# Making the weight sum S4 by an accumulating transfer instead of a VectorE addition, in four pairs of a feed-forward

## The chip, the cores and the metric

The kernel runs on one core of one Trainium2 chip. The metric is the device time of one execution in microseconds (us). Shorter is better. The kernel before has a median of 1458.25 us over 3 runs (1457.26 to 1460.52).

## The reference, cut to what matters

The kernel computes a two-layer encoder trunk on 512 tokens of width 1024 in float32. Each layer is a mixer, a cross-attention to a memory of 256 tokens, and a gated feed-forward with a short causal convolution; the change touches the feed-forward alone:

```python
def conv_ffn(xn, w_up, conv_w, conv_b, w_down):
    h = causal_depthwise_conv(xn @ w_up, conv_w) + conv_b
    g, u = jnp.split(h, 2, axis=-1)
    return (jax.nn.gelu(g) * u) @ w_down
```

w_up is 1024 x 5632 (D_FF is 2816), so g and u have 22 blocks of 128 columns each. There is one such feed-forward in each of the two layers.

## The kernel before, in words

**Pairs.** The feed-forward works on 22 pairs. Pair p is block p of g with block p of u: two weight blocks, A1 and A2, of 128 x 1024 elements, each stored as two halves of 512 columns (A11 and A12, A21 and A22). Pair 0 is computed plainly (`plain`, line 1703). Pairs 1 to 21 are computed by `seven` (line 1723), a scheme with seven half-size products instead of eight, which needs sums of the weight halves: S1 = A21 + A22, S2 = A11 + S1, S4 = S2 + A12, and the sum of A11 and A21.

**Sums and splits.** The tile `sa` is loaded with A11 and A21 by SyncE's queue (line 1736), and GpSimd's queue then adds A2 onto it by an accumulating transfer (`onto`, line 1732; used at line 1737). A1 is loaded into `raw` (line 1738), A22 into `ra` (line 1739). VectorE makes S2 in a tile `sb` (line 1753) and later S4 in place, in the same tile (line 1759). Each weight that a product uses is first split into two float32r parts: ScalarE casts it (the high part, line 1747) and VectorE subtracts (the low part, line 282). S4 may be made only when both parts of S2 have been made, since it overwrites S2. Five such splits belong to a pair: w3 (A1 whole), w2 (S2), w1 (`sa` whole), w22 (A22), w4 (S4); w3 and w1 serve two products each.

**Products.** Lines 1795 to 1810 give the products P1, P5, P6, P2, P7, P3, P4. Each is 12 matmuls of 256 columns (four blocks, three matmuls each, lines 291 to 293). P3 reads S4's parts, P6 reads S2's. Between them ScalarE and VectorE pass results on: ScalarE writes P6's bank with minus P1 before P6 may start (the seed, line 1786), keeps a copy of P6 (u2, line 1790) before P7 may overwrite it, and a copy of P5 (u5); VectorE subtracts these (line 1793), P4 waiting for the subtraction after P7. A tail then scales, convolves and gates the pair: ScalarE starts the convolution (line 1669), VectorE adds two taps to each half (line 1676), ScalarE does the gelu (line 1684), VectorE the product with u (line 1686), and the result is split again (lines 1690 and 282). From pair 5 on, products of the down projection of earlier pairs are put between (`fill`).

**Buffers.** There are three `raw` and three `sa` tiles, two `sb` and two `ra` tiles, and one pair of part tiles each for S2, S4 and A22.

**What sets the order.** A planner (`Sched`, line 150) is given every step with an engine, an estimated duration, its dependencies, a due time and the buffers that it takes, and writes the steps of each engine in the order in which they come up in its plan; the framework then lays the instructions out on each engine. A transfer of `onto` counts in the plan 0.0029 us per column on GpSimd, and its data 6.0 us after that. The load of the first table of the gelu on ScalarE is no step of the plan. On the chip every engine executes its own instructions strictly in this order; an instruction whose input is missing holds up all behind it on its engine.

Of the kernel before, what the change touches and what calls it, by code (L numbers as in the profile page):

```python
# [14 lines left out]
ALU = mybir.AluOpType  # L15
# [50 lines left out]
class Plan:  # L66
# [11 lines left out]
    def add(self, fn, dur=0.0, deps=(), prio=None, take=(), free=(), chain=(), pre=(), after=0.0, order=(), load=(), st=None):  # L78
        it = Item(fn, dur, [d for d in deps if d is not None], len(self.items) if prio is None else prio, take, free, chain, pre, after, order, load, st)
        it.n = len(self.items)  # L80
        self.items.append(it)
        return it
# [154 lines left out]
class Builder:  # L237
# [1269 lines left out]
    def ffn_steps(self, layer, mp):  # L1507
# [5 lines left out]
        add = sc.add  # L1513
        tt = lambda n: 0.055 + 1.06e-3 * n
# [22 lines left out]
        def load(st, tag, src, cols, at, dur=0.0017):  # L1537
            def fn():
                to = raw_tile(st, tag)[:, :cols]
                nc.sync.dma_start(to.rearrange("p (a b) -> p a b", a=2) if len(src.shape) == 3 else to, src)  # L1540

            return add("SP", dur * cols, fn, (), at, [(tag, st)], (), 4.0)

        def parts(st, off=0):
            st["wh"], st["wl"] = self.parts(off)
# [79 lines left out]
        def small_(tag):  # L1625
            both = self.til(self.kp, tag, (P, 1088), F32R, bufs=1)
            return both[:, OFF : OFF + 512], both[:, OFF + 512 : OFF + 1024]
# [95 lines left out]
        def seven(p, fill):  # L1723
            st, sa, sb, r2, f1, f3, s2, s4, a22 = ({} for _ in range(9))
            at = clock[0]
            A1, A2 = t["up"][layer, p], t["up"][layer, 22 + p]
            tt_ = nc.vector.tensor_tensor
# [3 lines left out]
            def onto(out, src, cols, deps, due):  # L1731
                return add("POOL", 0.0029 * cols, lambda: nc.gpsimd.dma_start(out(), src(), accum_op=ALU.add), deps, due, (), (), 6.0)  # L1732

            SB = lambda: sb["sb"][:]
            soon = 40.0 if p < 5 else 0.0
            b1 = load(sa, "sa", up2[p][:, :, :512], 1024, at - 20.0 - soon, 0.0 if soon else 0.0017)
            b1 = onto(lambda: sa["sa"][:], lambda: A2, 1024, [b1], at - 16.0 - soon)
            l2 = load(r2, "raw", A1, 1024, at - 12.0)
            l1 = load(a22, "ra", A2[:, 512:], 512, at - 6.0)

            def small(s, tag):
                s["wh"], s["wl"] = small_(tag)

            def split(s, cols, deps, due, alloc, take, raw, free=()):
                def hi():
                    alloc()
                    nc.scalar.copy(s["wh"][:, :cols], raw())  # L1747

                h = add("ACT", act(cols), hi, deps, due - 3.0, take)
                return add("DVE", tt(cols), lambda: self.sub(s["wl"][:, :cols], raw(), s["wh"][:, :cols]), [h], due - 2.0, (), free)  # L1750
# [1 line left out]
            def s2_():  # L1752
                tt_(out=raw_tile(sb, "sb")[:], in0=sa["sa"][:, 512:], in1=r2["raw"][:, :512], op=ALU.add)

            b2 = add("DVE", tt(512), s2_, [b1, l2], at - 5.0, [("sb", sb)])
            w3 = split(f3, 1024, [l2], at, lambda: parts(f3, OFF), [("h", f3)], lambda: r2["raw"][:])
            w2 = split(s2, 512, [b2], at, lambda: small(s2, "s2"), [("s2", s2)], SB)
            w1 = split(f1, 1024, [b1], at + 1.0, lambda: parts(f1, OFF), [("h", f1)], lambda: sa["sa"][:])
            b4 = add("DVE", tt(512), lambda: tt_(out=SB(), in0=SB(), in1=r2["raw"][:, 512:], op=ALU.add), [w2], at - 1.5)
            w22 = split(a22, 512, [l1], at + 4.0, lambda: small(a22, "a22"), [("a22", a22)], lambda: a22["ra"][:], [("ra", a22)])  # L1760
            w4 = split(s4, 512, [b4], at + 5.0, lambda: small(s4, "s4"), [("s4", s4)], SB, [("sb", sb)])
            joined([w1, b2], at, [("sa", sa)])
# [533 lines left out]
```

## Time and profile before

| what | value |
|---|---|
| median of 3 runs (lowest to highest) | 1458.25 us (1457.26 to 1460.52) |
| the profiled execution's own time | 1458.17 us |
| its span, first to last instruction | 1456.4 us |
| matmul engine (PE) busy | 1441.7 us (99% of the span) |
| VectorE (DVE) busy | 1225.6 us (84%) |
| ScalarE (ACT) busy | 986.1 us (68%) |
| GpSimd (POOL) busy | 73.3 us (5%) |
| TensorE clock granted | 0.999 |
| transfers' share of 16 engines: SyncE's queue, GpSimd's queue | 35.1%, 10.7% |

The profiled execution's time is its span and 1.8 us around it, and lies 0.08 us under the median. Pairs 1 to 5 of the first layer lie at about 417 to 467 us of the span, those of the second layer 703.27 us later, with the same instructions. A row of a timeline gives the start in us, the duration, the engine, the line, the operation, what it writes and reads, and in brackets the idle time before it with what ended it. Starts tell more than durations: each engine begins an instruction before the one ahead has drained, so the distance of two starts is what an instruction costs when the engine is not waiting. PE's busy share hides its halts for the same reason, since the modelled end of a matmul reaches past the start of the next.

### The profile page before, as it was taken

What the parts mean: (1) busy time and instruction counts of PE and PEld (TensorE: products, weight loads), DVE (VectorE), ACT (ScalarE), POOL (GpSimd) and SP (SyncE); (2) the same over time, 40 slices, a digit from 0 to 9 for tenths busy, and PEclk for the clock granted to TensorE, in tenths of its full rate; (3) what the DMA queues carried; (4) which work ended last, traced back from release to release, by engine and by line L of the source; (5) the groups of instructions that cost most, each with busy time, mean ns of one, the idle gap of its engine ahead of it and who ended that gap; (6) DMA issues with size and microseconds to landing.
All of it is one profiled execution on the core that took longest, in us unless ns stands there. A gap on an engine that the chain in (4) does not pass through costs nothing.

```text
span 1456.4 us, 24072 instructions
## 1 busy us (share of the span) xinstructions
PE 1441.7 (99%) x9019; PEld 1279.8 (88%) x9019; DVE 1225.6 (84%) x2223; ACT 986.1 (68%) x1776; POOL 73.3 (5%) x116
## 2 busy tenths in 40 slices
PE   9999999999999999999999999999999999999998
PEld 7888787998899999999888888889988999999987
DVE  7789987867899988889669988887779998888974
ACT  7689666655677777777547665566566777777764
POOL 0001120000000000000000100000000000000000
PEclk9999999999999999999999999999999999999999
DMA  5222336752246666562233332656414666666422
GB/s 200 87 74 73 117 119 199 171 177 88 94 128 163 183 158 161 150 163 74 84 101 109 109 110 65 204 142 189 131 48 119 160 179 172 156 160 156 105 67 79
DMA packets 70628, 190.24 MB, mean 131 GB/s; under 512 B 7520, under 2 KB 7520, under 8 KB 70512
## 3 DMA queue, kind: packets, MB, share of 16 engines
q1 hardware_dynamic: 62736, 162.17, 35.1%
q0 software_dynamic: 7200, 26.22, 10.7%
q8 instruction: 70, 1.15, 0.3%
q14 instruction: 46, 0.38, 0.1%
q10 hardware_dynamic: 576, 0.33, 0.1%
HBM read 186.56 MB, written 2.13 MB: 130 GB/s over the span
## 4 chain that ended last, share of the span: by engine, by line
PE 82%; DVE 10%; ACT 4%; issue 2%; DMA 1%; POOL 0%; DVEq 0%; SPq 0%; POOLq 0%; ACTq 0%
PE acc L291 15%; PE acc L292 15%; PE acc L293 14%; PE w L293 6%; PE w L291 6%; PE w L292 6%; PE s L293 3%; PE s L291 3%; PE s L292 3%; PE acc L352 2%; PE acc L354 2%; PE acc L353 2%; DVE wl L282 2%; DMA sa<-in_xq_dram 1%; DVE x L771 1%
## 5 line engine op out<-in xcount | busy, mean ns | idle before, releaser
L282 DVE TENSOR_TENSOR wl<-raw,wh 128x1024 fp32r<-128x1024 f32 (+3 forms) x181 | 213.9, 1182 | 41.2 <-ACT wh L285 32.3
L291 PE MATMUL acc<-xh,wh 128*128 128x256 f32 (+1 forms) x624 | 206.8, 331 | 0.1
L293 PE MATMUL acc<-xh,wl 128*128 128x256 f32 (+1 forms) x624 | 205.7, 330 | 0.1
L292 PE MATMUL acc<-xl,wh 128*128 128x256 f32 (+1 forms) x624 | 205.5, 329 | 0.0
L285 ACT CAST wh<-raw 128x1024 fp32r<-128x1024 f32 (+1 forms) x123 | 126.6, 1034 | 84.6 <-PE acc L292 43.0
L1676 DVE SCALAR_TENSOR_TENSOR c<-hs,vec,c 128x512 f32<-128x512 f32 x176 | 130.5, 749 | 15.9 <-ACT c L1669 14.0
L291 PEld LDWEIGHTS acc<-xh,wh 128*128 128x128 f32 x624 | 117.2, 188 | 12.1 <-ACT v L1917 0.6
L293 PEld LDWEIGHTS acc<-xh,wl 128*128 128x128 f32 x624 | 117.1, 188 | 12.0 <-DVE wl L282 0.5
L292 PEld LDWEIGHTS acc<-xl,wh 128*128 128x128 f32 x624 | 117.2, 188 | 11.5
L293 PE MATMUL w<-ah,wl 128*128 128x512 f32 x304 | 119.1, 392 | 0.0
L292 PE MATMUL w<-al,wh 128*128 128x512 f32 x304 | 118.6, 390 | 0.0
L291 PE MATMUL w<-ah,wh 128*128 128x512 f32 x304 | 118.5, 390 | 0.0
L282 DVE TENSOR_TENSOR wl<-sa,wh 128x1024 fp32r<-128x1024 f32 x52 | 63.6, 1222 | 17.0 <-ACT wh L1747 15.6
L1669 ACT ACTIVATE c<-hs,vec 128x512 f32<-128x512 f32 x88 | 71.2, 816 | 9.6 <-DVE hs L1816 8.2
L1747 ACT CAST wh<-sa 128x1024 fp32r<-128x1024 f32 x42 | 44.0, 1049 | 35.4 <-PE w L292 30.4
L293 PEld LDWEIGHTS w<-ah,wl 128*128 128x128 f32 x304 | 57.1, 188 | 12.0
L291 PEld LDWEIGHTS w<-ah,wh 128*128 128x128 f32 x304 | 57.1, 188 | 10.0 <-ACT w L1584 0.2
L292 PEld LDWEIGHTS w<-al,wh 128*128 128x128 f32 x304 | 57.0, 188 | 9.8
L282 DVE TENSOR_TENSOR s<-sb,s 128x512 fp32r<-128x512 f32 x92 | 63.1, 686 | 2.2 <-ACT s L285 0.3
L1554 ACT CAST wh<-dr 128x512 fp32r<-128x512 f32 x64 | 39.7, 621 | 34.1 <-PE w L292 32.2
L1732 POOL DMA_DIRECT2D sa<-in_up_dram x42 | 35.9, 855 | 515.7 <-DMA sa<-in_up_dram 173.9
L291 PE MATMUL acc<-mem,wh 128*128 128x256 f32 (+1 forms) x192 | 61.5, 320 | 0.0
(534 smaller groups left out, 4667.8 us busy)
## 6 DMA issues: line engine op xcount, KB each, us to landing
raw<-in_up_dram SPq DMA_DIRECT2D x46, 512.0 KB, 3.5
sa<-in_up_dram SPq DMA_DIRECT2D x42, 512.0 KB, 4.3
sa<-in_up_dram POOLq DMA_DIRECT2D x42, 512.0 KB, 5.7
dr<-in_down_dram SPq DMA_DIRECT2D x64, 256.0 KB, 2.7
ra<-in_up_dram SPq DMA_DIRECT2D x42, 256.0 KB, 3.0
raw<-in_xk_dram SPq DMA_DIRECT2D x16, 512.0 KB, 3.6
raw<-in_wo_dram SPq DMA_DIRECT2D x16, 512.0 KB, 3.5
raw<-in_xv_dram SPq DMA_DIRECT2D x16, 512.0 KB, 3.4
```

The source lines that it names most:

```text
L282: self.nc.vector.tensor_tensor(out=lo, in0=v, in1=hi.bitcast(F32), op=ALU.subtract)
L285: self.nc.scalar.copy(hi, v)
L291: mm(out, wh, xh, start=first, stop=False, skip_group_check=parts)
L292: mm(out, wh, xl, start=False, stop=False, skip_group_check=parts)
L293: mm(out, wl, xh, start=False, stop=last, skip_group_check=parts)
L352: mm(ps, xh[k][:, ts], wh[:, ws], start=(k == 0), stop=False)
L353: mm(ps, xh[k][:, ts], wl[:, ws], start=False, stop=False)
L1554: nc.scalar.copy(st["wh"][:, :cols], st[tag][:, :cols])
L1669: nc.scalar.activation(st["c_"][:, j, :], hs()[:, j, 2:514], AF.Identity, scale=self.col("cw", (layer * 3 + 2) * 44 + blk), bias=self.col( ...
L1676: nc.vector.scalar_tensor_tensor(out=c, in0=hs()[:, j, n : n + 512], scalar=w, in1=c, op0=ALU.mult, op1=ALU.add)
L1732: return add("POOL", 0.0029 * cols, lambda: nc.gpsimd.dma_start(out(), src(), accum_op=ALU.add), deps, due, (), (), 6.0)
L1747: nc.scalar.copy(s["wh"][:, :cols], raw())
```

## The change

For pairs 2 to 5 of both layers S4 is no longer made by VectorE from `raw`; GpSimd issues an accumulating transfer that adds A12 from HBM (128 x 512 elements, 256 KB) onto S2's tile once both parts of S2 are made. In the same pairs S2, its split and S4 are due 2.0 us earlier in the plan.

```diff
+            ahead = 2.0 if p in (2, 3, 4, 5) else 0.0
-            b2 = add("DVE", tt(512), s2_, [b1, l2], at - 5.0, [("sb", sb)])
+            b2 = add("DVE", tt(512), s2_, [b1, l2], at - 5.0 - ahead, [("sb", sb)])
...
-            w2 = split(s2, 512, [b2], at, lambda: small(s2, "s2"), [("s2", s2)], SB)
+            w2 = split(s2, 512, [b2], at - ahead, lambda: small(s2, "s2"), [("s2", s2)], SB)
...
-            b4 = add("DVE", tt(512), lambda: tt_(out=SB(), in0=SB(), in1=r2["raw"][:, 512:], op=ALU.add), [w2], at - 1.5)
+            if p in (2, 3, 4, 5):
+                b4 = onto(SB, lambda: A1[:, 512:], 512, [w2], at - 1.5 - ahead)
+            else:
+                b4 = add("DVE", tt(512), lambda: tt_(out=SB(), in0=SB(), in1=r2["raw"][:, 512:], op=ALU.add), [w2], at - 1.5)
```

Behind the change line numbers from 1755 on are larger by 1 to 4 (the seed is 1790, u2 and u5 are 1794). The planner also reorders the steps around. Three places, all in the first layer; the second has the same rows.

ScalarE at pair 2, before: the cast of S4 (`s4`) stands ahead of the first pair's convolution and of pair 2's seed (`acc2`); the table load and the gelu of pair 0 (`c`) come behind the seed.

```order
L1803 COPY hs00_4587<-acc1_954_4722 128x256
L1747 CAST s4_967_4828<-sb_959_4756 128x512
L1669 ACTIVATE c_968_4832<-hs01_4588,vec_103 128x512
L1747 CAST wh_970_4849<-raw_940_4660 128x1024
L1786 ACTIVATE acc2_972_4865<-acc1_969_4834 128x256
L1684 ACT_TABLE_LOAD
L1684 ACTIVATE c_968_4832<-c_968_4832 128x512
L1810 COPY hs00_4587<-acc3_958_4754 128x256
```

ScalarE at the same place after the change, with pair 2's u5 and the cast of pair 3's S2 (`s2`) behind.

```order
L1807 COPY hs00_4587<-acc1_955_4723 128x256
L1669 ACTIVATE c_966_4828<-hs01_4588,vec_103 128x512
L1747 CAST wh_968_4845<-raw_940_4660 128x1024
L1747 CAST s4_975_4901<-sb_953_4719 128x512
L1684 ACT_TABLE_LOAD
L1684 ACTIVATE c_966_4828<-c_966_4828 128x512
L1790 ACTIVATE acc2_971_4862<-acc1_967_4831 128x256
L1794 COPY u5_973_4884<-s_970_4849 128x256
L1747 CAST s2_974_4898<-sb_961_4775 128x512
```

The cast of S4 went behind two longer steps, and the table load, the gelu and pair 2's seed now stand behind that cast. On PE, P6 of pair 2 stands after P1 and P5 of pair 2 and 8 of the 12 matmuls of P4 of pair 1.

ScalarE at pair 5 before, where `s4_1028` is S4 of pair 5, `acc3_1027` its bank of P6 (seed, then u2) and `c_1020` the tail of pair 3.

```order
L1684 ACTIVATE c_1020_5217<-c_1020_5217 128x512
L1747 CAST a22_1026_5271<-ra_999_5075 128x512
L1810 COPY hs01_4588<-acc2_1008_5139 128x256
L1786 ACTIVATE acc3_1027_5277<-acc0_1025_5258 128x256
L1747 CAST s4_1028_5292<-sb_1021_5219 128x512
L1790 COPY u2_1030_5310<-acc3_1027_5277 128x256
```

ScalarE at pair 5 after the change (`s4_1041` is S4, `acc3_1026` the bank of P6, `c_1023` the tail of pair 3).

```order
L1790 ACTIVATE acc3_1026_5256<-acc0_1022_5222 128x256
L1747 CAST s4_1041_5372<-sb_1016_5208 128x512
L1684 ACTIVATE c_1023_5235<-c_1023_5235 128x512
L1747 CAST a22_1029_5292<-ra_1004_5100 128x512
L1814 COPY hs01_4588<-acc2_1007_5120 128x256
L1794 COPY u5_1030_5309<-s_1028_5279 128x256
L1690 CAST ah_1031_5312<-c_1023_5235 128x512
L1794 COPY u2_1033_5328<-acc3_1026_5256 128x256
```

The cast of S4 moved ahead of the gelu of pair 3 and of the cast of its product, and u2 of pair 5 now stands behind all of them.

GpSimd's queue after the change; before it held the transfers onto `sa` alone, in the same order.

```order
L1732 DMA sa_949_4693<-in_up_dram 128x1024
L1732 DMA sb_953_4719<-in_up_dram 128x512
L1732 DMA sa_972_4864<-in_up_dram 128x1024
L1732 DMA sb_961_4775<-in_up_dram 128x512
L1732 DMA sa_988_4984<-in_up_dram 128x1024
L1732 DMA sb_990_5003<-in_up_dram 128x512
L1732 DMA sa_1009_5153<-in_up_dram 128x1024
L1732 DMA sb_1016_5208<-in_up_dram 128x512
```

The four new transfers (onto `sb`, pairs 2 to 5) stand between those onto `sa` of pairs 4 to 7, each of which is issued three pairs ahead.

## The prediction

> **What bounds the kernel now.** I read the page first: the engines' busy time, then the chain of work that ended last.
>
> ```profile
> PE 1441.7 (99%) x9019; PEld 1279.8 (88%) x9019; DVE 1225.6 (84%) x2223; ACT 986.1 (68%) x1776; POOL 73.3 (5%) x116
> ...
> PE 82%; DVE 10%; ACT 4%; issue 2%; DMA 1%; POOL 0%; DVEq 0%; SPq 0%; POOLq 0%; ACTq 0%
> ```
>
> The matrix engine sets the time nearly everywhere. An edit on VectorE is worth only what it takes from PE's halts, and costs only the new halts that it makes. So I cut the stretch of pairs 1 to 5 of the first layer into windows (start and end, then busy us and instructions of PE, weight loads, DVE, ACT, POOL, then the granted clock, the transfers' share and GB/s).
>
> ```profile
> 417.00:427.00 10.00, 9.80 (x86) 9.55 (x84) 8.29 (x13) 7.90 (x14) 0.88 (x1) 1.00 0.42 86
> 427.00:437.00 10.00, 9.86 (x86) 9.86 (x87) 10.00 (x15) 8.71 (x16) 0.85 (x1) 1.00 0.65 174
> 437.00:447.00 10.00, 9.59 (x84) 9.39 (x83) 10.00 (x17) 7.49 (x14) 0.86 (x1) 1.00 0.58 156
> 447.00:457.00 10.00, 9.70 (x84) 9.39 (x83) 10.00 (x15) 7.15 (x14) 0.85 (x1) 1.00 0.61 154
> 457.00:467.00 10.00, 9.89 (x77) 9.18 (x77) 10.00 (x17) 7.17 (x13) 0.86 (x1) 1.00 0.67 178
> ```
>
> From 427 on VectorE is busy without a gap while PE has lost little: here alone VectorE is as full as PE, and the halts are in PE's timeline.
>
> ```profile
> 425.27 0.28 PE L291 MATMUL acc<-xh,wh 128*128 128x256 f32 x1
> ...
> 426.52 0.28 PE L293 MATMUL acc<-xh,wl 128*128 128x256 f32 x1
> 427.14 0.39 PE L291 MATMUL acc<-kv,a 128*128 128x256 f32 x1 [0.34 <-DVE hs L1793]
> ...
> 443.47 0.28 PE L293 MATMUL acc<-kv,wl 128*128 128x256 f32 x1
> 444.15 0.38 PE L291 MATMUL s<-xh,s 128*128 128x256 f32 x1 [0.41 <-ACT u L1790]
> ...
> 448.70 0.28 PE L292 MATMUL acc<-xl,wh 128*128 128x256 f32 x1
> 449.28 0.38 PE L291 MATMUL acc<-kv,s 128*128 128x256 f32 x1 [0.30 <-ACT acc L1786]
> ...
> 459.12 0.40 PE L292 MATMUL w<-al,wh 128*128 128x512 f32 x1
> 459.63 0.39 PE L291 MATMUL acc<-kv,s 128*128 128x256 f32 x1
> ```
>
> The first two rows are the first and last matmul of one product, 11 steps: 1.25 / 11 = 0.113 us each, a product of 12 takes 1.36, and a 512-column matmul costs two steps, 0.227. Beyond that pitch the halts are 0.62 - 0.11 = 0.51, 0.68 - 0.11 = 0.57, 0.58 - 0.11 = 0.47 and 0.51 - 0.23 = 0.28. The first matmul behind a halt is also longer by 0.11 (0.39 against 0.28). Layer 0: 1.83 + 4 x 0.11 = 2.27 us. The second layer has the same places 703.27 us later; the row that differs most is the third.
>
> ```profile
> 1152.56 0.38 PE L291 MATMUL acc<-kv,s 128*128 128x256 f32 x1 [0.15 <-ACT acc L1786]
> ```
>
> It waited 0.15 less than in layer 0, so I take 2.12 for this layer: 4.39 us in both layers is what the change can win here.
>
> **What the change removes.** Four VectorE additions per layer. VectorE's rows around the first give the prices as distances of starts.
>
> ```profile
> 422.74 0.68 DVE L282 TENSOR_TENSOR s<-sb,s 128x512 fp32r<-128x512 f32 x1
> 423.34 0.68 DVE L1713 TENSOR_TENSOR hs<-acc,rb 128x512 f32<-128x512 f32 x1
> 423.94 0.68 DVE L1759 TENSOR_TENSOR sb<-sb,raw 128x512 f32<-128x512 f32 x1
> 424.54 0.42 DVE L1793 TENSOR_TENSOR hs<-s,u 128x256 f32<-128x256 f32 x1
> 424.87 0.74 DVE L1676 SCALAR_TENSOR_TENSOR c<-hs,vec,c 128x512 f32<-128x512 f32 x1
> 425.53 1.22 DVE L282 TENSOR_TENSOR wl<-sa,wh 128x1024 fp32r<-128x1024 f32 x1
> 426.67 0.42 DVE L1793 TENSOR_TENSOR hs<-acc,u 128x256 f32<-128x256 f32 x1
> ```
>
> 512 columns cost 0.60, 256 columns 0.33, a tap 0.66, a 1024-wide subtraction 1.14. A layer loses 4 x 0.60 = 2.40 us of a VectorE that is full there. That is more than each halt alone (at most 0.57), so I credit all four as gone: minus 4.39. What is late next, where they go, is the new waits.
>
> **What it adds: the transfer's landing.** No row shows a 256 KB accumulating transfer. The near ones are GpSimd's 512 KB ones (issue instruction; landing, last figure, in two windows), the queue's packets, and SyncE's plain loads.
>
> ```profile
> 418.76 0.88 POOL L1732 DMA_DIRECT2D sa<-in_up_dram  x1 [13.52 <-DMA sa<-in_up_dram]
> 431.21 0.85 POOL L1732 DMA_DIRECT2D sa<-in_up_dram  x1 [11.57 <-DVE c L1676]
> ...
> sa<-in_up_dram POOLq DMA_DIRECT2D x1, 512.0 KB, 5.4
> sa<-in_up_dram POOLq DMA_DIRECT2D x42, 512.0 KB, 5.7
> q0 software_dynamic: 7200, 26.22, 10.7%
> raw<-in_up_dram SPq DMA_DIRECT2D x46, 512.0 KB, 3.5
> ra<-in_up_dram SPq DMA_DIRECT2D x42, 256.0 KB, 3.0
> ```
>
> The first two answer to the issue at 418.76 and to all 42. Below, it cannot be less than half of 5.4, 2.7 us; above, a transfer twice as large takes 5.7. Between: q0's packets took 0.107 x 16 x 1456.4 / 7200 = 0.35 us; one transfer is 128 of them (26.22 MB / 7200 is 3.6 KB, and 512 KB are 128 rows of 4 KB), 8 per engine, 2.8 us. Half the bytes save half of that, 1.4, so 5.4 - 1.4 = **4.0 us**; I take it, and call it d. SyncE's rows, where half the size saves only 0.5, say 4.9. GpSimd itself waited 13.5 and 11.6 us ahead of the transfers shown and these are issued three pairs ahead, so the four new issues of some 0.9 us delay nothing.
>
> [...]
>
> **First new wait: P6 of pair 2.** ScalarE before, at that place:
>
> ```profile
> 424.78 0.62 ACT L1747 CAST s<-sb 128x512 fp32r<-128x512 f32 x1
> 425.31 0.82 ACT L1669 ACTIVATE c<-hs,vec 128x512 f32<-128x512 f32 x1
> 426.02 1.04 ACT L1747 CAST wh<-raw 128x1024 fp32r<-128x1024 f32 x1
> 426.96 0.37 ACT L1786 ACTIVATE acc<-acc 128x256 f32<-128x256 f32 x1
> 427.35 1.28 ACT L1684 ACT_TABLE_LOAD   x1
> 428.64 0.64 ACT L1684 ACTIVATE c<-c 128x512 f32<-128x512 f32 x1
> 429.18 0.35 ACT L1810 COPY hs<-acc 128x256 f32<-128x256 f32 x1
> 429.43 0.62 ACT L1747 CAST a<-ra 128x512 fp32r<-128x512 f32 x1
> ```
>
> Starts give: cast 0.53, convolution 0.71, wide cast 0.94, seed 0.39, table load 1.29, gelu 0.54, copy 0.25. After the change the S4 cast comes third, so ScalarE reaches it at 424.78 + 0.71 + 0.94 = 426.4. Its input: S2's low part ends at 422.74 + 0.68 = 423.42; I put 0.3 from there to the issue (an estimate: GpSimd is idle, and one semaphore lies between), and d: 427.72. Behind the cast are queued the table load, the gelu and then the seed that P6 needs: 0.53 + 1.29 + 0.54 + 0.39 = 2.75, and 0.2 for two semaphores (an estimate, between nothing and the 0.3 above): P6 could start at 430.65. PE gets there at 426.52 + 0.11 + 1.36 (P5 of pair 2) + 8 x 0.113 (of P4 of pair 1) = 428.9. PE waits 1.75 + 0.11 = **1.86 us**.
>
> **Second: P7 of pair 5.** It needs u2, which stands behind the S4 cast of pair 5. There is one buffer for S2's parts, so the S2 cast of pair 3 waits for the end of P6 of pair 2, 430.65 + 1.36 = 432.0, and its subtraction starts at 432.7. From there to the end of S2's subtraction of pair 5 stand 33 VectorE rows that I take as back to back (busy 10.00 of 10.00 above): 14 x 0.60 + 7 x 1.14 + 8 x 0.66 + 4 x 0.33 = 23.0: 455.8. Issue and landing: 460.1. Then ScalarE's row of cast 0.53, gelu 0.54, cast of A22 0.53, copy 0.25, u5 0.25, cast of the product 0.53, u2 0.25 and again 0.2 for semaphores: 3.1, so 463.2. PE, at its pitch from P6 of pair 2 through 23 products and four matmuls more (0.45), is there at 430.65 + 31.3 + 0.45 = 462.4. PE waits 0.8 + 0.11 = **0.9 us**.
>
> By the same walk the S4 cast of pairs 3 and 4 lands 0.25 to 1.0 us ahead of its use: no halt. SyncE's loads of `raw` may go earlier, since S4 no longer holds it, which meets transfers with a share of 0.6 above: nothing.
>
> **The sum**, against the profiled execution's own 1458.17 (0.08 under the median of 1458.25): 1458.17 - 4.39 + 2 x (1.86 + 0.9) = **1459.3 us**. With d at 2.75, P6 waits 0.63 per layer and P7 nothing: 1455.0. With 5.7 both waits grow by 1.7: 1458.17 - 4.39 + 2 x (3.58 + 2.6) = 1466.1. A microsecond of d costs 4 (two places, two layers).
>
> **Rivals.**
>
> A. *VectorE's relief alone counts*: the landing takes no more than 2.8 us, or the walk above has a microsecond of slack that I missed. 1455.0. For it: VectorE at 10.00 of 10. Against: every landing shown is 3.0 or more, and the seed stands behind the table load.
>
> B. *The landing hardly depends on the size, or is late.* It decides P6 of pair 2 and P7 of pair 5, and from d = 4.5 on the kernel is slower by more than 0.2%. SyncE's rows (0.5 saved) give 4.9 and 1462.9; no saving gives 1466.1. One of the transfers of 512 KB, issued in the window from 441.4 us on, took this:
>
> ```profile
> sa<-in_up_dram POOLq DMA_DIRECT2D x1, 512.0 KB, 7.0
> ```
>
> so a late one costs 1.6 more at its place. Against: the packets' own 2.8 us must shrink with the bytes.
>
> [...]
>
> D. *The old halts stay.* Two of the four are put down to ScalarE (u and the seed), not VectorE, and nothing is taken from it. Then 1458.17 + 5.5 = 1463.7. Against: ScalarE was busy 7.2 to 8.7 of 10, and waits for VectorE's results itself.
>
> **How the numbers follow.** About 0.2%, 2.9 us, is what a measurement of this kernel can tell from no change. Forecast, within it: 0.46. A: 0.14, faster. B: 0.32, C: 0.03, D: 0.05, all slower: 0.40. The likeliest single case is the forecast, 1459.3, with its own range from 1457.3 (d = 3.5) to 1461.2 (d = 4.5). The range goes from A's time to 1465.5, just under B's end, which leaves out the full 5.7 and what is beyond, and gains above 4.39: about 2 in 10.
>
> **What would show it.** [...] P6 of pair 2: a PE halt of about 1.75 near 430.6, put down to ScalarE's seed, with the table load between the S4 cast and the seed. P7 of pair 5: a halt of 0.8 near 463, put down to ScalarE's u2. Relief: no halt at the four places above, and VectorE under 10.00 of 10 in the windows. I am wrong if the S4 cast's landing is not what the halts wait for, or if pairs 3 and 4 halt too.

## The result, and the profile after

The changed kernel takes 1466.35 us (median of 6 runs, 1464.6 to 1469.75) against 1458.97 us before, measured beside it (6 runs, 1457.26 to 1461.39). The ratio is 1.0056, with a 95% interval of 1.0043 to 1.0068: slower by 7.4 us by the medians and by 8.2 us by the ratio, 0.85 us beyond the upper end of the predicted range. Two executions behind the numbers of this document took far longer than all others, 2405.8 us (with pair 5 alone) and 2045.8 us (the kernel before), and the ratios leave them out.

The page of the changed kernel, the same two lines as before, busy time and then the chain that ended last:

```profile
PE 1440.7 (98%) x9019; PEld 1279.3 (87%) x9019; DVE 1222.5 (84%) x2215; ACT 985.2 (67%) x1776; POOL 81.1 (6%) x124
...
PE 77%; DVE 12%; ACT 4%; DMA 3%; issue 3%; SPq 0%; POOL 0%; DVEq 0%; ACTq 0%; POOLq 0%
```

VectorE has 8 instructions less and GpSimd 8 more, as the change says. What is new stands in the chain: DMA went from 1% to 3% of the span, and PE's own share fell from 82% to 77%. The windows of the first layer (columns as before; this execution is 1.4 us later at pair 2 than the one of before) show where:

```profile
427.00:437.00 10.00, 8.41 (x74) 8.21 (x73) 8.26 (x13) 7.25 (x13) 1.70 (x2) 1.00 0.72 176
437.00:447.00 10.00, 10.00 (x90) 10.00 (x89) 10.00 (x16) 8.01 (x16) 1.32 (x2) 1.00 0.73 176
447.00:457.00 10.00, 8.75 (x76) 8.54 (x75) 8.29 (x12) 5.54 (x11) 1.24 (x2) 1.00 0.91 206
457.00:467.00 10.00, 8.69 (x77) 8.49 (x75) 8.44 (x15) 6.28 (x13) 1.20 (x2) 1.00 0.66 151
```

VectorE, busy 10.00 of 10 in these windows before, is now idle for 1.6 to 1.7 us in three of them, and PE and ScalarE are idle with it: a wait for one thing stops all three. PE's timeline names the places, P6 of pair 2, P7 of pair 4, P7 of pair 5 and P6 of pair 6 in the first layer, then P6 of pair 2, P7 of pair 5 and P6 of pair 6 in the second (in brackets the idle time before the first matmul of the product):

```profile
432.03 0.38 PE L291 MATMUL acc<-kv,s 128*128 128x256 f32 x1 [1.59 <-ACT acc L1790]
...
455.89 0.39 PE L291 MATMUL acc<-kv,wh 128*128 128x256 f32 x1 [1.25 <-ACT u L1794]
...
467.82 0.39 PE L291 MATMUL acc<-kv,wh 128*128 128x256 f32 x1 [2.13 <-ACT u L1794]
...
480.81 0.38 PE L291 MATMUL acc<-kv,s 128*128 128x256 f32 x1 [0.39 <-ACT acc L1790]
...
1138.67 0.38 PE L291 MATMUL acc<-kv,s 128*128 128x256 f32 x1 [1.51 <-ACT acc L1790]
...
1173.24 0.38 PE L291 MATMUL acc<-kv,wh 128*128 128x256 f32 x1 [1.90 <-ACT u L1794]
...
1186.24 0.39 PE L291 MATMUL acc<-kv,s 128*128 128x256 f32 x1 [0.39 <-ACT acc L1790]
```

The bracket counts from the modelled end of the matmul ahead. From start to start, less the pitch of 0.113 and with the 0.11 of the first slow matmul, a halt is 0.27 longer: 1.87, 1.53, 2.40 and 0.67 us in the first layer, 1.78, 2.18 and 0.66 in the second, **11.1 us** in all. Counted in the same way, the kernel before halts 4.9 us in these two stretches: the four halts per layer of the prediction, and 0.27 us at P7 of pair 6. So the halts account for 6.2 of the 7.2 us by which this execution's span is longer; the rest arises where the change does nothing, 1.4 us more ahead of pair 2 and 0.3 us less between the layers. All the new halts are put down to ScalarE's seed (`acc`, line 1790) or its copy u2 (`u`, line 1794). What ScalarE did ahead of the first and the third of them:

```profile
429.14 0.62 ACT L1747 CAST s<-sb 128x512 fp32r<-128x512 f32 x1 [1.22 <-DMA sb<-in_up_dram]
429.78 1.28 ACT L1684 ACT_TABLE_LOAD   x1
431.08 0.63 ACT L1684 ACTIVATE c<-c 128x512 f32<-128x512 f32 x1
431.61 0.37 ACT L1790 ACTIVATE acc<-acc 128x256 f32<-128x256 f32 x1
...
464.77 0.62 ACT L1747 CAST s<-sb 128x512 fp32r<-128x512 f32 x1 [3.53 <-DMA sb<-in_up_dram]
465.30 0.63 ACT L1684 ACTIVATE c<-c 128x512 f32<-128x512 f32 x1
465.83 0.60 ACT L1747 CAST a<-ra 128x512 fp32r<-128x512 f32 x1
466.34 0.36 ACT L1814 COPY hs<-acc 128x256 f32<-128x256 f32 x1
466.60 0.37 ACT L1794 COPY u<-s 128x256 f32<-128x256 f32 x1
466.87 0.63 ACT L1690 CAST ah<-c 128x512 fp32r<-128x512 f32 x1
467.38 0.38 ACT L1794 COPY u<-acc 128x256 f32<-128x256 f32 x1
```

The S4 cast waits 1.22 and 3.53 us for the transfer's data, and what PE needs stands three and six instructions behind it. The transfers themselves, GpSimd's issues at pairs 3 and 4 with those onto `sa` just ahead of them, and the landings (last figure) of pairs 2, 3, 4 and 5 of the first layer:

```profile
432.52 0.86 POOL L1732 DMA_DIRECT2D sa<-in_up_dram  x1 [6.51 <-DVE sb L1753]
435.47 0.84 POOL L1732 DMA_DIRECT2D sb<-in_up_dram  x1 [2.10 <-DVE s L282]
444.68 0.86 POOL L1732 DMA_DIRECT2D sa<-in_up_dram  x1 [8.37 <-DVE c L1676]
446.53 0.84 POOL L1732 DMA_DIRECT2D sb<-in_up_dram  x1 [0.99 <-DVE s L282]
...
sb<-in_up_dram POOLq DMA_DIRECT2D x1, 256.0 KB, 4.0
sb<-in_up_dram POOLq DMA_DIRECT2D x1, 256.0 KB, 5.1
sb<-in_up_dram POOLq DMA_DIRECT2D x1, 256.0 KB, 6.8
sb<-in_up_dram POOLq DMA_DIRECT2D x1, 256.0 KB, 4.4
```

In the second layer they took 3.9, 5.0, 5.3 and 4.8 us. Pair 2's transfers are alone on the queue, and so is pair 5's in the first layer: the one onto `sa` ahead of it was issued 5.7 us earlier and took 5.4. Each of the others was issued before the one ahead of it had landed. The four halts of before (at P4 of pair 1 and three later products) are gone; PE comes to those places later now.

### The profile page after: what moved, and what is told of

It reads as the page before. It is cut to its first block, busy times and chain, and to the rows that moved or that the text cites. A ratio compares the mean times of both kernels' runs of the same rounds, so it can differ in the third digit from the quotient of the medians.

```text
span 1463.6 us, 24054 instructions
## 1 busy us (share of the span) xinstructions
PE 1440.7 (98%) x9019; PEld 1279.3 (87%) x9019; DVE 1222.5 (84%) x2215; ACT 985.2 (67%) x1776; POOL 81.1 (6%) x124
## 3 DMA queue, kind: packets, MB, share of 16 engines
HBM read 188.66 MB, written 2.13 MB: 130 GB/s over the span
## 4 chain that ended last, share of the span: by engine, by line
PE 77%; DVE 12%; ACT 4%; DMA 3%; issue 3%; SPq 0%; POOL 0%; DVEq 0%; ACTq 0%; POOLq 0%
PE acc L291 14%; PE acc L292 14%; PE acc L293 14%; PE w L293 6%; PE w L291 6%; PE w L292 6%; PE s L291 3%; PE s L293 3%; PE s L292 3%; DVE wl L282 2%; PE acc L352 2%; PE acc L354 2%; PE acc L353 2%; DMA sb<-in_up_dram 1%; DVE c L1676 1%
## 5 line engine op out<-in xcount | busy, mean ns | idle before, releaser
L1747 ACT CAST s<-sb 128x512 fp32r<-128x512 f32 x84 | 52.0, 619 | 32.1 <-DMA sb<-in_up_dram 13.3
```

## The experiments

**Is it the landing, or the new order?** Four kernels. In the first the transfers are left out and all else stays (a few steps change places with their neighbours in this and in other experiments, since the framework lays the instructions out anew):

```diff
-                b4 = onto(SB, lambda: A1[:, 512:], 512, [w2], at - 1.5 - ahead)
+                b4 = add("POOL", 0.0029 * 512, lambda: None, [w2], at - 1.5 - ahead, (), (), 6.0)
```

> The changed kernel with the transfers onto S2's tile left out in pairs 2 to 5 (S4 is then S2, so A12 is missing from the sum); due times and plan as changed. Landing theory (PE halts because ScalarE's S4 cast waits for the transfer, with the seed or u2 queued behind it): the halts at P6 of pair 2, P7 of pair 4 and P7 of pair 5 go, but for some 0.5 us at P6 of pair 2 per layer that the table load ahead of the seed leaves; 1454 to 1457 us. Order theory (the earlier due times and the new order of ScalarE's work cost the time, whenever the data come): 1463 to 1467 us.

Measured: 1458.55 us (1457.89 to 1460.04), ratio 1.0002 (0.9993 to 1.001). The whole loss is gone, so it is the transfer's, by its landing or its traffic, and not the order's. But the time is not below the kernel before either, where 1454 to 1457 us had been expected, although VectorE does 2.4 us less per layer. PE still halts at P6 of pair 2 and at P6 of pair 7 in both layers:

```profile
429.19 0.39 PE L291 MATMUL acc<-kv,s 128*128 128x256 f32 x1 [0.72 <-ACT acc L1790]
...
490.96 0.38 PE L291 MATMUL acc<-kv,s 128*128 128x256 f32 x1 [0.60 <-ACT acc L1790]
...
1194.11 0.38 PE L291 MATMUL acc<-kv,s 128*128 128x256 f32 x1 [1.13 <-ACT acc L1790]
```

The second takes the addition out of the kernel before and puts nothing in its place:

```diff
-            b4 = add("DVE", tt(512), lambda: tt_(out=SB(), in0=SB(), in1=r2["raw"][:, 512:], op=ALU.add), [w2], at - 1.5)
+            b4 = add("DVE", tt(512), (lambda: None) if p in (2, 3, 4, 5) else (lambda: tt_(out=SB(), in0=SB(), in1=r2["raw"][:, 512:], op=ALU.add)), [w2], at - 1.5)
```

> The kernel before with VectorE's addition for S4 left out in pairs 2 to 5 (S4 is then S2), nothing in its place. Relief theory (VectorE's 2.4 us per layer were what the old halts waited for): all four old halts per layer shrink, 4.4 us less, about 1454.5 us. Rival (two of the four halts are ScalarE's own): halts at P6 and P5 of later pairs stay, 1457 to 1459 us.

Measured: 1457.38 us (1456.72 to 1459.96), ratio 0.9993 (0.9984 to 1.0002). The gain is at most 2.3 us of the 4.4 and more likely one, and the interval includes none. The three later halts of each layer are gone, among them the two put down to ScalarE. The one at P4 of pair 1, put down to VectorE, stays, and others come, such as one at P6 of pair 7:

```profile
427.18 0.38 PE L291 MATMUL acc<-kv,a 128*128 128x256 f32 x1 [0.40 <-DVE hs L1793]
...
490.45 0.39 PE L291 MATMUL acc<-kv,s 128*128 128x256 f32 x1 [0.29 <-ACT acc L1786]
```

The first is the old halt. VectorE's rows ahead of it show why it is as long as it was:

```profile
423.92 0.74 DVE L1676 SCALAR_TENSOR_TENSOR c<-hs,vec,c 128x512 f32<-128x512 f32 x1
...
426.71 0.41 DVE L1793 TENSOR_TENSOR hs<-acc,u 128x256 f32<-128x256 f32 x1
```

A tap, 0.66 us, came into the place of the addition, 0.60 us, and the subtraction that P4 waits for starts at 426.71 against 426.67 before. So this kernel does not show what that halt would be with less work ahead of it.

The third has the due times without the transfer, the fourth the transfer without the due times:

```diff
-            if p in (2, 3, 4, 5):
+            if False:
...
-                b4 = add("DVE", tt(512), lambda: tt_(out=SB(), in0=SB(), in1=r2["raw"][:, 512:], op=ALU.add), [w2], at - 1.5)
+                b4 = add("DVE", tt(512), lambda: tt_(out=SB(), in0=SB(), in1=r2["raw"][:, 512:], op=ALU.add), [w2], at - 1.5 - ahead)
```

> The earlier due times alone: S2, its split and S4 are due 2.0 us earlier in pairs 2 to 5, S4 still made by VectorE. Landing theory: no landing is waited for, so within 2 us of the kernel before, 1457 to 1461 us. Order theory: most of the loss is here already, 1463 to 1467 us.

```diff
-            ahead = 2.0 if p in (2, 3, 4, 5) else 0.0
+            ahead = 0.0
```

> The transfers alone, with the due times of the kernel before. Landing theory: S2's low part comes no earlier, so the landing is as late or later and the halts at pairs 2, 4 and 5 stay or grow, 1464 to 1470 us. Order theory: without the earlier due times the loss goes, about 1459 us.

Measured: 1457.76 us, ratio 0.9997 (0.9988 to 1.0006), and 1464.27 us (1463.28 to 1468.45), ratio 1.0044 (1.0032 to 1.0057). The due times cost nothing that can be measured; the transfer alone costs most of the loss. With the kernel without transfers, which has the new order and no loss, the order theory falls.

**How the parts add up.** The gelu's table load, 1.28 us, stands between the S4 cast and the seed of pair 2. A gelu of a small tile of zeros (`gz`) ahead of that cast moves it into ScalarE's idle time:

```diff
+        gz = mp.tile([P, 8], F32, name=f"gz{layer}")
+        nc.gpsimd.memset(gz[:], 0.0)
...
                 def hi():
                     alloc()
+                    if p == 2 and due == at + 5.0:
+                        nc.scalar.activation(gz[:], gz[:], AF.Gelu_apprx_tanh)
                     nc.scalar.copy(s["wh"][:, :cols], raw())
```

> The changed kernel with the gelu's table loaded before the S4 cast of pair 2 (a gelu of a 128 x 8 tile of zeros just ahead of that cast, where ScalarE idled 1.2 us for the transfer). Landing theory: only 0.53 + 0.54 + 0.39 us stand between the landing and P6, so its halt falls from 1.87 to about 0.6 per layer and the end of P6 of pair 2 moves everything behind it with it: 2.6 us less than the changed kernel, about 1463.8 us. Rival (what sets pair 5 is not P6 of pair 2 but VectorE's row): the 2.6 us come back at P7 of pair 5, 1466 us.

Measured: 1466.21 us (1465.09 to 1468.02), ratio 1.0055 (1.0042 to 1.0067): no gain. P6 of pair 2 still halted 1.50 us (it fell by 0.4 and not by 1.3, since P6 now stood ahead of P4 of pair 1 on PE and was due earlier), and P7 of pair 5 grew to 2.97, as the rival had it:

```profile
430.58 0.39 PE L291 MATMUL acc<-kv,s 128*128 128x256 f32 x1 [1.23 <-ACT acc L1794]
...
466.56 0.38 PE L291 MATMUL acc<-kv,wh 128*128 128x256 f32 x1 [2.70 <-ACT u L1798]
```

The next three make the change for some pairs only, by the list of pairs in its two lines (here pair 2; then 5; then 3 and 4):

```diff
-            ahead = 2.0 if p in (2, 3, 4, 5) else 0.0
+            ahead = 2.0 if p in (2,) else 0.0
...
-            if p in (2, 3, 4, 5):
+            if p in (2,):
```

> The change for pair 2 alone. Landing theory: only the halt at P6 of pair 2, 3.65 us in both layers, which covers the old halt of 0.62 per layer just ahead of it: 1460 to 1462 us. Rival (pair 2's late landing sets off the halts of pairs 4 and 5): 1464 to 1467 us.

> The change for pair 5 alone. Landing theory: P7 of pair 5 halts behind the S4 cast, 2 to 4 us per layer (VectorE lacks the relief of the pairs ahead, so S2's low part of pair 5 comes no earlier), less old halts of up to 0.4 behind it: 1462 to 1466 us. Rival (pair 5 waits only because pairs 2 to 4 are late): 1458 to 1460 us.

> The change for pairs 3 and 4 alone, where the prediction saw 0.25 to 1.0 us of slack. Landing theory: a halt only where a landing is over 5.3 us, so 1457 to 1460 us. Rival (the transfers themselves slow the queue and the loads, wherever they stand): 1461 to 1464 us.

Measured: pair 2 alone 1460.93 us, ratio 1.0017 (1.0009 to 1.0026); pair 5 alone 1462.12 us, ratio 1.0025 (1.0015 to 1.0034), at the low edge of what was expected; pairs 3 and 4 alone 1467.18 us, ratio 1.0061 (1.0047 to 1.0074). With pair 2 alone, P6 of pair 2 halts 1.63 and 1.81 us. With pair 5 alone the profiled execution, 1461.13 us, bears the expectation out only in part: P7 of pair 5 halts 0.97 us in the second layer, where the transfer took 5.9 us, and not at all in the first, where it took 4.6 (in this order u2 stands directly behind the S4 cast); P7 of pair 6 halts 0.87 and 0.74 us where it halted 0.27 before. Pairs 3 and 4 were a miss: two pairs cost as much as all four. In this order the seeds of pairs 3 and 4 stand behind the S4 casts, as that of pair 2 does in the changed kernel. The halts at P6 of pairs 3 and 4, both layers, and ScalarE from the S4 cast to the seed ahead of the first (three steps left out):

```profile
442.47 0.38 PE L291 MATMUL acc<-kv,s 128*128 128x256 f32 x1 [2.04 <-ACT acc L1790]
...
453.41 0.39 PE L291 MATMUL acc<-kv,s 128*128 128x256 f32 x1 [1.54 <-ACT acc L1790]
...
1148.76 0.39 PE L291 MATMUL acc<-kv,s 128*128 128x256 f32 x1 [1.86 <-ACT acc L1790]
...
1160.86 0.39 PE L291 MATMUL acc<-kv,s 128*128 128x256 f32 x1 [2.70 <-ACT acc L1790]
```

```profile
440.22 0.62 ACT L1747 CAST s<-sb 128x512 fp32r<-128x512 f32 x1 [3.19 <-DMA sb<-in_up_dram]
...
442.05 0.37 ACT L1790 ACTIVATE acc<-acc 128x256 f32<-128x256 f32 x1
```

So the theory was sharpened: not the landing costs, but what stands behind the waiting cast in ScalarE's queue. S4 itself is needed only at P3, three products after P6.

**Taking the queue away.** In pairs 2 to 5 the S4 cast is held behind u2 of its own pair, in the plan and in ScalarE's order; its transfer, its landing and its wait stay. Then neither seed nor u2 can queue behind it:

```diff
-                    nc.scalar.copy(s["wh"][:, :cols], raw())
+                    with ExitStack() as es:
+                        if s is s4 and p in (2, 3, 4, 5):
+                            es.enter_context(self.tc.issue_after(st["u2i"].ins))
+                        nc.scalar.copy(s["wh"][:, :cols], raw())
...
-            w4 = split(s4, 512, [b4], at + 5.0, lambda: small(s4, "s4"), [("s4", s4)], SB, [("sb", sb)])
...
-                nc.scalar.copy(st[tag][:], bank(n_)())
+                st[tag + "i"] = nc.scalar.copy(st[tag][:], bank(n_)())
...
             u2 = add("ACT", act(256), lambda: kept("u2", "Y"), [p6], clock[0], [("u2", bu2)])
+            w4 = split(s4, 512, [b4, u2] if p in (2, 3, 4, 5) else [b4], at + 5.0, lambda: small(s4, "s4"), [("s4", s4)], SB, [("sb", sb)])
```

> The changed kernel with one thing held: in pairs 2 to 5 the S4 cast stands behind the copy u2 of the same pair in ScalarE's order; seed and u2 no longer queue behind the landing. Queue theory (what costs is not the landing itself but the seed and u2 queued behind the cast that waits for it): the halts at P6 of pair 2 and P7 of pairs 4 and 5 go, what is left is VectorE's relief of about 1 us: 1456 to 1459 us. Rival (the landing is too late for P3 too, or for VectorE's row): halts come back at P3, 1461 us or more.

The control does the same to the kernel before, without transfers:

> Control: the kernel before, S4 made by VectorE, with its S4 casts of pairs 2 to 5 held behind u2 in the same way. Queue theory: nothing waits for a landing, so nothing to win; 1457 to 1460 us. Rival (the new order itself is the better one): 1453 to 1456 us.

Measured: 1459.99 us (1458.03 to 1462.14), ratio 1.0014 (1.0005 to 1.0024), and for the control 1458.15 us, ratio 1.0001 (0.9992 to 1.001). With the same transfers, landing in 3.8 to 6.0 us, 6.4 us come back by the medians and 6.1 by the ratios, some four fifths of the loss, and the order as such wins nothing. The time is still 1 us above what was expected, and the rival was right in a part: S4's low part now comes late for P3 of pair 5. What is left of halts in the first layer, at P6 of pair 2, within P3 of pair 5 and at P6 of pair 6 (the second layer has the same three, and two more of 0.75 and 0.37 us at P4 of pair 3 and P6 of pair 5):

```profile
428.52 0.39 PE L291 MATMUL acc<-kv,s 128*128 128x256 f32 x1 [0.21 <-ACT acc L1792]
...
467.17 0.39 PE L293 MATMUL s<-xh,s 128*128 128x256 f32 x1 [0.55 <-DVE s L282]
...
476.02 0.39 PE L291 MATMUL acc<-kv,s 128*128 128x256 f32 x1 [0.59 <-ACT acc L1792]
```

Two more kernels tell the seed from u2, and the queue from the traffic. In one the cast is held behind the seed only, so that u2 still queues behind it (`v` and its instruction in place of u2 in the diff above); in the other the costly pairs 3 and 4 alone are held behind u2:

> The changed kernel with the S4 casts of pairs 2 to 5 held behind the seed of the same pair only; u2 still stands behind the cast. Queue theory: the halt at P6 of pair 2 shrinks to 0.5 us or less, those at P7 of pair 5 (and 4 where a landing is late) stay at 2 to 3 us per layer: 1463 to 1466 us. Rival (only the seed of pair 2 counts, pair 5 follows from it): 1459 to 1461 us.

> The change for pairs 3 and 4 alone, as in the run before of that kind (1467.2 us), but with their S4 casts held behind u2. Queue theory: the halts at P6 of pairs 3 and 4 go, 1458 to 1460 us. Rival (the transfers' traffic, or S4 itself being late for P3): 1463 us or more.

Measured: 1464.02 us (1459.92 to 1466.44), ratio 1.0034 (1.0021 to 1.0046), and 1458.84 us, ratio 0.9999 (0.999 to 1.0008). The second is clear: 8.3 us are gone with the queue, so for these two pairs the transfers' traffic as such costs nothing that can be measured. The first is so by its times only. Its profiled execution took 1461.74 us; there P6 of pair 2 halts 0.48 us as expected, but P7 of pair 5 only 0.5 us in one layer and not at all in the other. Where its other executions lose up to 5 us more was not seen; a late landing in front of u2 would do it.

**What sets the landing.** In the first the transfers onto `sa` of pairs 5 to 8 are left out, in the second the new transfers carry half the columns:

```diff
-            b1 = onto(lambda: sa["sa"][:], lambda: A2, 1024, [b1], at - 16.0 - soon)
+            if p in (5, 6, 7, 8):
+                b1 = add("POOL", 0.0029 * 1024, lambda: None, [b1], at - 16.0 - soon, (), (), 6.0)
+            else:
+                b1 = onto(lambda: sa["sa"][:], lambda: A2, 1024, [b1], at - 16.0 - soon)
```

> The changed kernel with the transfers onto sa left out in pairs 5 to 8 (A2 is then missing from their sums), which stand between those onto S2's tile on GpSimd's queue. Queue sharing theory (a landing over 4.0 us comes from the 512 KB transfer ahead of it on the same queue): landings of pairs 3, 4 and 5 fall from 5.1, 6.8 and 4.4 to 4.0 to 4.4, and the halt at P7 of pair 4 goes; 1463 to 1465 us. Rival (SyncE's loads slow them): landings stay near 5 to 6 us, 1466 us.

```diff
-                b4 = onto(SB, lambda: A1[:, 512:], 512, [w2], at - 1.5 - ahead)
+                b4 = add("POOL", 0.0029 * 512, lambda: nc.gpsimd.dma_start(SB()[:, :256], A1[:, 512:768], accum_op=ALU.add), [w2], at - 1.5 - ahead, (), (), 6.0)
```

> The changed kernel with half the columns in each new transfer, 128 KB (256 columns of A12 are missing from S4). Packet theory of the prediction (1.9 us fixed, the rest in proportion to the bytes): landing 2.9 to 3.0 us alone on the queue, and 4 us less in all if every microsecond of it counts at two places per layer: 1462 us. Rival (the landing hardly depends on the size): 3.6 us or more and 1465 to 1466 us.

Measured: 1463.25 us (1460.11 to 1463.64) and 1463.87 us (1462.43 to 1467.67). The first is within what was expected, the second above (1462 us). The landings of pairs 3, 4 and 5 without the `sa` transfers, and that of pair 2 with half the columns (a row each, first layer):

```profile
sb<-in_up_dram POOLq DMA_DIRECT2D x1, 256.0 KB, 5.0
sb<-in_up_dram POOLq DMA_DIRECT2D x1, 256.0 KB, 3.9
sb<-in_up_dram POOLq DMA_DIRECT2D x1, 256.0 KB, 4.4
```

```profile
sb<-in_up_dram POOLq DMA_DIRECT2D x1, 128.0 KB, 3.1
```

Pair 4's landing, 6.8 us behind a transfer that had been issued 1.85 us earlier, falls to 3.9 and its halt goes: that one was the shared queue. Pair 3's stays at 5.0 and pair 5's at 4.4 (5.3 in the second layer), so for those the queue is not the cause. SyncE's loads are the rival; no run leaves them out, and the traces do not settle it: in the changed kernel their share of the engines was 31.6% during pair 3's 5.1 us, but 17.4% during pair 5's 4.4 us and 26.5% during pair 2's 4.0 us. The half transfer of pair 2 landed in 3.1 us: 128, 256 and 512 KB alone on the queue took 3.1, 3.9 (pair 2's in the changed kernel's second layer, pair 4's here) and 5.4 us. Those of pairs 3 to 5 took 3.7 to 5.2 us at half the size too. The time of that kernel says nothing on the price of a microsecond, since here a wide cast came between the S4 cast and the table load, and P6 of pair 2 halted longer (2.16 us) although the data came 0.8 us earlier. The 1.9 us fixed of the expectation for the half transfer are an estimate that no run shows; the prediction's own figures leave 5.4 - 2.8 = 2.6 us and would give 2.6 + 0.7 = 3.3.

**What is left.** Pair 5 without the change, and the table load ahead of pair 1's S4 cast, each added to the held order; then the table load alone in the kernel before; then both without pair 5:

> The change for pairs 2 to 4 with the S4 casts held behind u2, pair 5 as before. Queue theory: without pair 5's late S4 at P3 (0.7 to 0.9 us per layer) 1 to 2 us under the run with pairs 2 to 5, 1457.5 to 1459.5 us. Rival (what is lost there comes back at another product): 1460 us.

> Pairs 2 to 5 with the S4 casts held behind u2, and the gelu's table loaded ahead of pair 1's S4 cast. Queue theory: the 0.5 us halt left at P6 of pair 2 in each layer goes, 1458.5 to 1459.5 us. Rival (VectorE's row sets the time of pairs 3 to 5 anyway): 1460 us, as without it.

> Control: the kernel before with the gelu's table loaded ahead of pair 1's S4 cast, nothing else. If the table load alone made the last run's gain: 1456.5 to 1457.5 us. Queue theory: in the kernel before the seed stands ahead of the table load, so the load holds up no product, only VectorE's product of pair 0 behind the gelu: 1457.5 to 1458.5 us.

> Pairs 2 to 4 by transfer, their S4 casts held behind u2, and the gelu's table loaded ahead of pair 1's S4 cast; pair 5 as before. Queue theory: the 0.5 us halt at P6 of pair 2 goes, about 1 us under the same without the table, 1456.5 to 1457.5 us. Rival (pair 5's relief is what the last run gained by): 1458 us.

| kernel | median, us | ratio (95% interval) |
|---|---|---|
| pairs 2 to 5, behind u2 | 1459.99 | 1.0014 (1.0005 to 1.0024) |
| pairs 2 to 4, behind u2 | 1458.10 | 1.0000 (0.9991 to 1.0009) |
| pairs 2 to 5, behind u2, table early | 1456.85 | 0.9987 (0.9979 to 0.9996) |
| pairs 2 to 4, behind u2, table early | 1456.91 | 0.9990 (0.9981 to 0.9999) |
| kernel before, table early | 1458.42 | 1.0000 (0.9991 to 1.0008) |

With the queue gone the table load counts for pairs 2 to 5: 3.1 us by the medians, more than the 1 us of halts at P6 of pair 2 that was expected. In the profiled executions the halts of the two stretches fall from 5.6 to 2.3 us, as those within P3 of pair 5 go too. For pairs 2 to 4 it counts 1.2 us, with intervals that overlap. In the kernel before it counts nothing, as the seed stands ahead of it there. In the fastest version, pairs 2 to 5 with the table early, pair 3's landings took 7.5 and 7.1 us, and P3 of pair 3, which reads that S4, does not halt: not even long landings cost anything there. The two versions with both edits are under the kernel before by about 0.1%, 1.5 and 1.2 us by the medians, which is near the 0.9 us that the kernel without the addition gave. No version here won more.

## Why the prediction was wrong, point by point

- **What bounds the kernel: right.** PE sets the time, and what the change moved in the profiled execution are PE's halts in pairs 1 to 6.
- **The landing of pair 2 and the halt at P6 of pair 2: right.** 4.0 and 3.9 us were measured against 4.0, issue 0.35 us behind S2's low part against 0.3, and halts of 1.87 and 1.78 against 1.86, with the table load in the chain as forecast.
- **The second halt failed.** The step is "P7 of pair 5 ... PE waits 0.8 + 0.11 = 0.9 us", with "the S4 cast of pairs 3 and 4 lands 0.25 to 1.0 us ahead of its use: no halt". Measured: 2.40 and 2.18 us at pair 5, 1.53 us at P7 of pair 4 in one layer. The mechanism, u2 behind the waiting cast, was right; the size was off, in the main because d = 4.0, which pair 2 has, was carried to the later transfers, which took 5.1, 6.8, 4.4 us, and 5.0, 5.3, 4.8. What made them longer is shown for pair 4 alone, the shared queue; for pairs 3 and 5 it stays open. In the second layer, counted from the start of P6 of pair 2, the data of pair 5 land at 31.45 us instead of 29.45. Of these 2.0 us, d gave 0.76; VectorE's row with its start 0.93 (it began 0.33 later, took 23.7 us and not 23.1); the issue 0.31 (0.61 us behind the low part). PE came 0.75 later too, so the halt grew by 1.25. With pair 4's, halts forecast at 0.9 x 2 measured 6.1 us: 4.3 us of the error.
- **A halt behind the change was not seen.** P6 of pair 6 halts 0.67 and 0.66 us, 1.3 us of the error. It is the same kind of queue without a transfer: in the new order the seed, at 480.39, stands behind pair 6's S4 cast, and that waits for VectorE's addition. Before, the seed stood ahead of it.

```profile
479.87 0.62 ACT L1747 CAST s<-sb 128x512 fp32r<-128x512 f32 x1 [1.53 <-DVE sb L1763]
```

- **What the halts leave open.** By the halts alone the time would be 1458.17 + 6.2 = 1464.4 us, inside the range. The 2 us from there to the median are not traced to the change: 1.1 us lie outside the two stretches, and most of the rest between the profiled execution and the median.
- **The credit of 4.39 us failed as a reason.** The old halts are gone in the changed kernel, as the sum has it, but in the shade of the new ones. Without any landing, leaving the addition out was worth 0.9 us (at most 2.3, perhaps nothing) from the kernel before and nothing in the new order, as other halts came in the place of the old. Rival D had that little is won, but not why: the two halts put down to ScalarE, which it said would stay, went, and the one put down to VectorE stayed.
- **Rival B** named the two places and the side. That its 1466.1 us is the measured time is luck: its reason, a landing that hardly depends on the size, is false for a transfer alone (3.1, 3.9 and 5.4 us for 128, 256 and 512 KB), and by it P6 of pair 2 would have halted 3.58 us, not 1.87. What it said of late landings is what happened. Halving 512 KB saved 1.4 to 1.5 us (5.4 to 4.0 and 3.9).
- **C**, given 0.03: no run shows a longer issue. The new issues took 0.84 to 0.88 us, with VectorE's rows back to back beside them in the first layer, against 0.88 and 0.85 in the kernel before. Rival A did not occur.
- **A microsecond of d costs 4**: not shown. The order of ScalarE changes with every edit and moves the price.

## What to carry to other kernels

Before a wait for a transfer is put on an engine, read what stands behind it in that engine's queue: here S4 had three products of time, but the next pair's inputs stood behind its cast, and holding the cast behind them won back four fifths of the loss with the same transfers. Price a landing from a transfer of that kind with neighbours on its queue, not from one alone: pair 4's took 6.8 us behind one and 3.9 without it. And relieving a full engine need not win the halts beside it: without the four additions 0.9 of 4.4 us were won here, and the halt put down to VectorE stayed. Take the engine's work out without a replacement, look whether the order stayed, and measure that first.

## What the runs showed of the hardware

Behind some long halts the matrix engine ran at about half its pace. In the kernel with the transfer and no due times, PE's matmuls behind a halt of 2.35 us, the row of the halt and then rows from 0.9 us on (start, duration):

```profile
431.71 0.38 PE L291 MATMUL acc<-kv,s 128*128 128x256 f32 x1 [2.35 <-ACT acc L1790]
...
432.63 0.31 PE L292 MATMUL acc<-kv,s 128*128 128x256 f32 x1
432.75 0.41 PE L293 MATMUL acc<-kv,s 128*128 128x256 f32 x1
432.95 0.42 PE L291 MATMUL acc<-kv,s 128*128 128x256 f32 x1
```

The distance of starts goes from 0.12 to 0.21 us, and the window of that stretch has a granted clock of 0.59 (the third figure from the end):

```profile
432.00:436.00 4.00, 4.00 (x24) 4.00 (x24) 1.47 (x4) 2.11 (x5) 0.42 (x1) 0.59 0.84 140
```

At half pace, 0.59 in 4.00 us stands for a stretch of 0.41 x 4.00 / 0.5 = 3.3 us, half of which, 1.6 us, is lost (an estimate from these two figures). A second one stands in the same profile behind a halt with an idle time of 3.43 us: 512-column matmuls start 0.40 to 0.43 us apart there and not 0.23, and the window of 468 to 472 us has a clock of 0.79. In two more kernels a window of 4 us has 0.63 (the table early, behind an idle time of 2.70 us) and 0.62 (without the transfers onto `sa`). A halt of the changed kernel with an idle time of 2.13 us was not followed by one: the window of 468 to 472 us has 1.00. With half the columns there was an idle time of 2.99 us, and the mean granted clock of that profile is 0.999, as in the changed kernel's; in the kernel with the transfer and no due times it is 0.995. Three of the changed kernel's six executions, of 1464.6, 1469.45 and 1469.75 us, have means of 0.996 and 0.997; they may have had such stretches, which is not shown. Nor do the runs show why one halt is followed by such a stretch and another is not.
